# First stage of a hybrid SSD and retention step: dummies of 512 columns, a transfer of their own for the condition vectors, modulation weights first in the queue, no paired modulation

## The chip, the cores and the metric

The kernel runs on one core of a Trainium2 chip. The metric is the device time of that core in microseconds (us). The kernel before takes 601.47 us, the median of three runs (601.31 to 603.59). Its engines are TensorE (PE in the profile, with PEld for its weight loads), VectorE (DVE), ScalarE (ACT), GpSimd (POOL) and SyncE (SP, which here only issues DMAs). ScalarE issues two DMAs too, on a queue of its own.

## The reference, cut to what matters

One layer works on 640 tokens of width 1024: 128 context tokens (modulated by the vector `c_ctx`) and 512 latent tokens (modulated by `c`). The stage that the change touches computes the first two lines below and the part `h @ w_in` for 512 of the columns.

```python
def _layer(x, cond, ...):
    mod = jax.nn.silu(cond) @ w_mod + b_mod
    shift, scale, gate = jnp.split(mod, 3, axis=-1)
    h = _rms(x, norm_pre_w) * (1 + scale[:, None, :]) + shift[:, None, :]
    out, s_ssd, s_ret = _mixer(h.astype(x.dtype), ...)    # begins with u = h @ w_in
    y = x + gate[:, None, :] * _rms(out, norm_post_w)
```

All the rest of the mixer (convolution, two bidirectional scans, gates, the output product with `w_out`) is untouched.

## The kernel before, in words

The tokens lie in five tiles of 128 (t = 0 is the context, t = 1 to 4 the latent tokens), the width in eight k-tiles of 128. The normalised and modulated activations are kept transposed, as a high and a low half (`hh`, `hl`); each product with a weight tile is three matmuls of 512 columns (high by high, high by low, low by high). The first stage fills `hh` and `hl` and at the same time multiplies them with the first 512 columns of `w_in`, into five banks of accumulators (`acc`). It ends when 120 such matmuls are done; then the first product named `gt` begins.

The stage is a list of steps in the string START, whose order is the order in which the program is written down. A letter is a step, the number its k-tile or token tile:

- L loads a token tile (512 KB), M a tile of modulation weights (1 MB), W a tile of `w_in` (256 KB). All go out on SP's queue.
- N squares a token tile on ScalarE and sums it (line 278), then GpSimd raises the sum to the power -1/2 (279). E scales a whole token tile on ScalarE, Q its first 128 columns on VectorE, R the other 896.
- A is the modulation product of a k-tile: eight matmuls with `silc` (SiLU of the condition vectors) as weights, and a copy `ms` on VectorE. B turns the result by two matmuls with the identity (`mod<-idt,ms`) and makes shift and scale (`ash`) on VectorE. P does A for two k-tiles in one bank.
- U and V split a weight tile into `w0h` (ScalarE) and `w0l` (VectorE).
- H transposes token tiles (PE `tr`), modulates them on ScalarE (`h`, line 355) and splits them on VectorE (`hh`, `hl`).
- G is the three matmuls of one token tile and one k-tile. Z are dummy matmuls on zeros: Z1 is four of 128 columns.

Three small tensors come first: `pk` (216 columns of vectors, the condition vectors in columns 0 to 15) and `idt` (the identity) on ScalarE's queue, and the tokens on SP's. `silc` is made of `pk` by one ScalarE and two VectorE instructions (267 to 270). Each engine works through its list in order; a DMA may be issued only when the transfer eight DMAs before it has landed, because eight semaphores go round.

Of the kernel before, what the change touches and what calls it, by code (L numbers as in the profile page):

```python
# [10 lines left out]
F32 = mybir.dt.float32  # L11
F32R = mybir.dt.float32r
AF = mybir.ActivationFunctionType
ALU = mybir.AluOpType
# [3 lines left out]
P = 128  # L18
D = 1024
KT = 8  # L20
# [5 lines left out]
Z0, XS0, B0, C0, DT0, Q0, K0, V0, G0 = 0, 1024, 2048, 2560, 3072, 3104, 3616, 4128, 5152  # L26


PK_CC, PK_C, PK_NPW, PK_BSH, PK_BSC = 0, 8, 16, 24, 32
# [12 lines left out]


START = """
L0 M0 L1 W0 L2 M1 W1 L3 L4 M2 W2
Z18 N0 E0 N1 A0 M3 Z2 B0 H0:0 U0 Q1 V0 W3 Z4 H0:1 N2 G0:0 Z1 G0:1 R1 Q2 R2 A1 M4 U1 H0:2 W4 N3 B1 G0:2 H1:012 V1 Z4 G1:012
Q3 A2 M5 H0:3 R3 N4 U2 W5 G0:3 H1:3 B2 V2 Q4 H0:4 G1:3 R4 H2:0123 G0:4 H1:4 A3 M6 G2:01 G1:4 H2:4 U3 W6 G2:23 B3 V3
P4 M7 H3:0123 G2:4 H3:4 U4 W7 B4 V4
G3:01 H4:0123 H4:4 U5 G3:234 B5 V5 C0
P6 G4:01 H5:0123 H5:4 U6 G4:234 B6 V6 F2  # L50
G5:01 H6:0123 H6:4 U7 G5:234 B7 V7 F2
G6:01 H7:0123 H7:4 F2 G6:234
G7:01234
"""
# [55 lines left out]
def body(ctx, tc, io):  # L110
    nc = tc.nc
    vec, act, pool, sp, pe = nc.vector, nc.scalar, nc.gpsimd, nc.sync, nc.tensor

    def sb(name, bufs=1, side=None):
        return ctx.enter_context(tc.tile_pool(name=name, bufs=bufs, side=side))

    const = sb("const")
# [8 lines left out]
    def mm(out, a, b, start, stop, big=False):  # L126
        r = pe.matmul(out, lhsT=a, rhs=b, start=start, stop=stop)  # L127
        if big:
            last["mm"] = getattr(r, "ins", r)

    def stt(out, in0, s, in1, op0=ALU.mult, op1=ALU.add, eng=vec):
        eng.scalar_tensor_tensor(out=out, in0=in0, scalar=s, in1=in1, op0=op0, op1=op1)  # L132

    def tt(out, a, b, op, eng=vec):
        return eng.tensor_tensor(out=out, in0=a, in1=b, op=op)  # L135

    def bank(name):
        return pi.tile([P, 512], F32, tag="i", name=name)


    pk = const.tile([P, PK_N], F32, name="pk")
    cst = const.tile([P, CN], F32, name="cst")
    idt = const.tile([P, P + 2], F32, name="idt")
    rope = const.tile([P, 4, 2, 64], F32, name="rope")
    act.dma_start(out=pk, in_=io["pk"])
    act.dma_start(out=idt, in_=io["idt"])
    tl = const.tile([P, 1], F32, name="tl")
# [6 lines left out]
    def pkc(base, n=0):  # L154
        return pk[:, base + n:base + n + 1]
# [87 lines left out]
    st_ = tc.alloc_tile_pool(name="st", bufs=1, side="right")  # L243
# [3 lines left out]
    wm_t, w0_t = {}, {}  # L247
# [16 lines left out]

    sc_ = st_.tile([P, KT, 32], F32, name="silc")
    th = st_.tile([P, 16], F32, name="thc")
    act.activation(th, pk[:, PK_CC:PK_CC + 16], AF.Tanh, scale=0.5)
    vec.memset(sc_, 0.0)
    stt(th, th, 1.0, pk[:, PK_CC:PK_CC + 16], ALU.add, ALU.mult)
    vec.tensor_scalar(sc_[:, :, 0:2], th.rearrange("p (c k) -> p k c", c=2), 0.5, None, op0=ALU.mult)  # L270
    bs1 = st_.tile([P, 8], F32, name="bs1")
    vec.tensor_scalar(bs1, pk[:, PK_BSC:PK_BSC + 8], 1.0, None, op0=ALU.add)
# [15 lines left out]
        eng.tensor_scalar(xs_t[t][:, q], xs_t[t][:, q], rs[:, t:t + 1], None, op0=ALU.mult)  # L288

    mods = {}  # L290
    wz = st_.tile([P, P], mybir.dt.bfloat16, name="wz")
    pool.memset(wz, 0.0)

    def warm(n):
        wps = bank("warm")
        for _ in range(4 * n):
            mm(wps[:, 0:P], wz, wz, True, True)

    def mod_a(kt):
        m = bank("mod")  # L300
# [15 lines left out]
    def low0(kt):  # L316
        hi = w0[kt][0]
        lo = st_.tile([P, 512], F32R, tag="w0l", name="w0l", bufs=3)
        tt(lo, w0_t.pop(kt), hi.bitcast(F32), ALU.subtract)
        w0[kt] = (hi, lo)  # L320

    ash_t, h_last = {}, {}

    def mod_pair(kt):
        m = bank("mod")
        for n in range(2):
            wm = wm_t.pop(kt + n)
            for k in range(KT):
                g = 32 * (k % 4)
                mm(m[g:g + 32, n * 256:n * 256 + 256], sc_[:, k, :], wm[:, k, :], k < 4, k >= 4)  # L330
        ms = st_.tile([P, 512], F32, tag="ms2", name="ms2")
        vec.tensor_copy(ms, m)
        for n in range(2):
            mods[kt + n] = (None, ms[:, n * 256:n * 256 + 256])

    def mod_b(kt):
        m, ms = mods.pop(kt)
        if m is None:
            m = bank("modb")
        mm(m[:, 256:258], ms[:, 0:P], idt[:, P:P + 2], True, True)  # L340
        mm(m[:, 258:260], ms[:, P:256], idt[:, P:P + 2], True, True)
        ash = ash_t[kt] = st_.tile([P, 4], F32, tag="ash", name="ash", bufs=3)
        vec.tensor_scalar(ash[:, 0:2], m[:, 256:258], pkc(PK_BSH, kt), None, op0=ALU.add)
        vec.tensor_scalar(ash[:, 2:4], m[:, 258:260], bs1[:, kt:kt + 1], pkc(PK_NPW, kt), op0=ALU.add, op1=ALU.mult)

    def h_tile(kt, ts):
        ash = ash_t[kt]
# [22 lines left out]
    def gemm0(kt, t):  # L370
# [5 lines left out]

    acc = [pg.tile([P, 512], F32, tag="g", name="acc0") for _ in range(5)]
    steps = {
        "M": load_wm, "W": load_w0, "L": load_x, "A": mod_a, "P": mod_pair, "U": high0, "V": low0, "B": mod_b, "N": norm_x,
        "E": all_x, "Q": first_x, "R": rest_x,  # L380
    }
    for op in START.split():
        k = int(op[1:].split(":")[0])
        if op[0] == "H":
            h_tile(k, [int(t) for t in op[3:]])
        elif op[0] == "G":
            for t in op[3:]:
                gemm0(k, int(t))
        elif op[0] == "Z":
            warm(k)  # L390
        elif op[0] == "F":
            feed(k, 0)
        elif op[0] == "C":
            sp.dma_start(out=cst, in_=io["cst"])
            sp.dma_start(out=rope, in_=io["rope"])
        else:
            steps[op[0]](k)
# [562 lines left out]
    for g in range(1, 4):  # L960
        n = clock["slot"]
# [5 lines left out]
    n = clock["slot"]  # L967
# [114 lines left out]
    n = clock["slot"]  # L1082
# [99 lines left out]
```

## Time and profile before

| What | Value |
|---|---|
| Median of three runs | 601.47 us |
| The profiled execution: its own time, and its span | 602.56 us, 600.7 us |
| PE busy / DVE / ACT / POOL | 583.8 / 415.8 / 338.2 / 30.8 us |
| First real matmul of PE (modulation of k-tile 0) | 7.72 us |
| First accumulating matmul | 11.50 us |
| End of the first stage (first `gt`) | 60.17 us |
| DMA rate, 5 to 25 us | 407 to 420 GB/s |

PE is busy for 97% of the span, but a dummy counts as busy too, and a matmul's time in a row is its passage through the array, longer than its share of the issue. What the stage costs is therefore read from the chain of waits, which runs back from the last instruction and names at each step what was waited for. Times are from the span's start.

### The profile page before, as it was taken

Reading aid. Unit: us, or ns where it says so; the run is one execution under the profiler, and the core shown is the slowest. Engines: PE = TensorE matmul, PEld = TensorE weight load, DVE = VectorE, ACT = ScalarE, POOL = GpSimd, SP = SyncE. Lnnn points to the kernel's source line nnn. Section 1 sums busy time; section 2 is a strip of 40 time slices with the busy share of each in tenths; the row PEclk is TensorE's granted clock in tenths of the full one; section 3 lists DMA queues with packets and bytes.
Section 4 is the critical chain, followed back from the end, with each engine's and each line's share of the span. In section 5 each row is a group of like instructions: output and inputs, shape, how many; then the busy total and the mean of one; then the engine's idle time right before and its main releaser. Section 6 shows DMA issues by size and latency. Waiting matters only on the chain.

```text
span 600.7 us, 11145 instructions
## 1 busy us (share of the span) xinstructions
PE 583.8 (97%) x3925; PEld 525.1 (87%) x3925; DVE 415.8 (69%) x938; ACT 338.2 (56%) x935; POOL 30.8 (5%) x112
## 2 busy tenths in 40 slices
PE   7999999999999999999999999999999999999995
PEld 6568989988999998899999888999999777788895
DVE  3648498756789865658897656799767855743665
ACT  5538246664666765465776546566755847262421
POOL 1000002100000010000011000000110000000010
PEclk9999999999999999999999999999999999999998
DMA  8983032643335533332563313355437676384032
GB/s 343 371 314 121 21 106 60 181 131 106 88 114 175 165 92 89 88 105 89 176 179 100 93 56 102 106 178 162 118 101 231 229 243 209 123 274 119 17 141 106
DMA packets 47639, 87.45 MB, mean 146 GB/s; under 512 B 5792, under 2 KB 18656, under 8 KB 46048
## 3 DMA queue, kind: packets, MB, share of 16 engines
q1 hardware_dynamic: 47296, 86.57, 45.5%
q8 instruction: 31, 0.51, 0.3%
q10 hardware_dynamic: 288, 0.18, 0.1%
q14 instruction: 24, 0.20, 0.1%
HBM read 75.03 MB, written 9.60 MB: 141 GB/s over the span
## 4 chain that ended last, share of the span: by engine, by line
PE 70%; DVE 8%; DMA 8%; ACT 7%; issue 4%; POOL 2%; SPq 0%; DVEq 0%; POOLq 0%; ACTq 0%
PE gw L127 24%; PE gc L127 15%; PE gt L127 9%; PE acc L127 5%; PE go L127 4%; DMA cf<-cumd 3%; DMA x<-x 2%; PE ss L127 2%; PE sfb L127 2%; DMA raw<-ws 1%; PE ry L127 1%; PE sy L127 1%; DVE SC L132 1%; DVE wlo L135 1%; PE st L809 1%
## 5 line engine op out<-in xcount | busy, mean ns | idle before, releaser
L135 DVE TENSOR_TENSOR wlo<-raw,whi 128x512 fp32r<-128x512 f32 (+1 forms) x120 | 82.1, 691 | 48.0 <-ACT whi L178 47.2
L178 ACT CAST whi<-raw 128x512 fp32r<-128x512 f32 (+1 forms) x120 | 73.6, 619 | 74.1 <-PE gw L127 45.6
L127 PE MATMUL gc<-hh,whi 128*128 128x320 f32 x384 | 96.8, 331 | 0.0
L127 PE MATMUL gc<-hl,whi 128*128 128x320 f32 x384 | 88.3, 310 | 0.0
L127 PE MATMUL gc<-hh,wlo 128*128 128x320 f32 x384 | 87.7, 310 | 0.0
L127 PEld LDWEIGHTS gc<-hh,whi 128*128 128x128 f32 x384 | 64.0, 189 | 1.1
L127 PEld LDWEIGHTS gc<-hl,whi 128*128 128x128 f32 x384 | 64.4, 188 | 0.1
L127 PEld LDWEIGHTS gc<-hh,wlo 128*128 128x128 f32 x384 | 64.1, 188 | 0.0
L127 PE MATMUL gw<-whi,hh 128*128 128x512 f32 x120 | 50.6, 421 | 0.8 <-ACT u L514 0.8
L127 PE MATMUL gw<-whi,hl 128*128 128x512 f32 x120 | 47.1, 392 | 0.0
L127 PE MATMUL gw<-wlo,hh 128*128 128x512 f32 x120 | 47.0, 391 | 0.0
L127 PE MATMUL gt<-whi,hh 128*128 128x256 f32 (+1 forms) x160 | 46.4, 290 | 0.0
L127 PE MATMUL gt<-wlo,hh 128*128 128x256 f32 (+1 forms) x160 | 45.8, 286 | 0.0
L127 PE MATMUL gt<-whi,hl 128*128 128x256 f32 (+1 forms) x160 | 45.8, 286 | 0.0
L892 ACT ACTIVATE m<-gu,dt 128x128 f32<-128x128 f32 x80 | 31.2, 390 | 16.4 <-DVE gu L135 14.6
L864 ACT ACTIVATE cf<-cf,dmc 128x128 f32<-128x128 f32 x80 | 26.5, 393 | 19.9 <-DMA cf<-cumd 19.9
L135 DVE TENSOR_TENSOR m<-m,cf 128x512 f32<-128x512 f32 x40 | 27.6, 689 | 8.8 <-ACT cf L893 7.6
L127 PE MATMUL gw<-whi,mrh 128*128 128x512 f32 x80 | 32.4, 404 | 0.0
L127 PE MATMUL gw<-wlo,mrh 128*128 128x512 f32 x80 | 31.3, 391 | 0.0
L867 ACT ACTIVATE cf<-cf,ncf 128x128 f32<-128x128 f32 x80 | 26.4, 394 | 8.5 <-DVE cf L135 8.5
L127 PEld LDWEIGHTS gt<-whi,hh 128*128 128x128 f32 x160 | 30.5, 191 | 0.7 <-issue 0.5
L893 ACT ACTIVATE cf<-gu,dt 128x128 f32<-128x128 f32 x80 | 31.0, 387 | 0.0
(238 smaller groups left out, 1334.7 us busy)
## 6 DMA issues: line engine op xcount, KB each, us to landing
raw<-ws SPq DMA_DIRECT2D x116, 256.0 KB, 2.8
cf<-cumd SPq DMA_DIRECT2D x20, 512.0 KB, 4.1
wm<-wm SPq DMA_DIRECT2D x8, 1024.0 KB, 9.1
mraw<-mixd SPq DMA_DIRECT2D x16, 320.0 KB, 3.8
ef<-ecumd SPq DMA_DIRECT2D x32, 128.0 KB, 3.4
wg<-wg SPq DMA_DIRECT2D x4, 1024.0 KB, 6.4
x<-x SPq DMA_DIRECT2D x5, 512.0 KB, 8.1
mixd<-rmix SPq DMA_DIRECT2D x20, 128.0 KB, 2.4
```

The source lines that it names most:

```text
L127: r = pe.matmul(out, lhsT=a, rhs=b, start=start, stop=stop)
L132: eng.scalar_tensor_tensor(out=out, in0=in0, scalar=s, in1=in1, op0=op0, op1=op1)
L135: return eng.tensor_tensor(out=out, in0=a, in1=b, op=op)
L178: act.copy(hi, raw)
L809: pe.transpose(o[:, n], src[:, s], ident)
L864: act.activation(cf[:, e, 1, q], cf[:, e, 1, q], AF.Identity, bias=dmc[:, c, h:h + 1])
L867: act.activation(cf[:, e, 0, q], cf[:, e, 0, q], AF.Exp, bias=ncf[:, c, h:h + 1])
L892: act.activation(m[:, e, q], gu[:, 0], AF.Copy, scale=dt[:, c, h:h + 1])
L893: act.activation(cf[:, e, 1, q], gu[:, 1], AF.Copy, scale=dt[:, c, 16 + h:17 + h])
```

## The change

The transfer of the 16 condition columns is made a DMA of its own (`cc`), ahead of `pk`; the two instructions on `thc` read it instead of `pk`. In START the first loads are now M0 L0 W0 L1 L2 in place of L0 M0 L1 W0 L2. The dummies become matmuls of 512 columns, one for each count of Z in place of four, with new counts. E0 is gone: token tile 0 is scaled by Q0 and R0 like the others. N1 and N2 now stand behind the first U0, Q0 and V0. P is gone; A4 to A7 are separate steps, one ahead of each H. The low half of a weight tile (V) is issued behind `ash` of its k-tile.

```diff
-L0 M0 L1 W0 L2 M1 W1 L3 L4 M2 W2
-Z18 N0 E0 N1 A0 M3 Z2 B0 H0:0 U0 Q1 V0 W3 Z4 H0:1 N2 G0:0 Z1 G0:1 R1 Q2 R2 A1 M4 U1 H0:2 W4 N3 B1 G0:2 H1:012 V1 Z4 G1:012
+M0 L0 W0 L1 L2 M1 W1 L3 L4 M2 W2
+Z14 A0 M3 Z2 B0 N0 U0 Q0 V0 W3 Z9 H0:0 N1 N2 Z3 G0:0 R0 Q1 R1 Z3 H0:1 Z2 A1 M4 U1 Q2 G0:1 R2 H0:2 W4 N3 B1 G0:2 V1 H1:012 N4 Z4 G1:012
...
-P4 M7 H3:0123 G2:4 H3:4 U4 W7 B4 V4
-G3:01 H4:0123 H4:4 U5 G3:234 B5 V5 C0
-P6 G4:01 H5:0123 H5:4 U6 G4:234 B6 V6 F2
+A4 M7 H3:0123 G2:4 H3:4 U4 W7 B4 V4
+A5 G3:01 H4:0123 H4:4 U5 G3:234 B5 V5 C0
+A6 G4:01 H5:0123 H5:4 U6 G4:234 B6 V6 F2
...
+    cc = const.tile([P, 16], F32, name="cc")
+    act.dma_start(out=cc, in_=io["pk"][:, PK_CC:PK_CC + 16])
     act.dma_start(out=pk, in_=io["pk"])
     act.dma_start(out=idt, in_=io["idt"])
...
-    act.activation(th, pk[:, PK_CC:PK_CC + 16], AF.Tanh, scale=0.5)
+    act.activation(th, cc, AF.Tanh, scale=0.5)
     vec.memset(sc_, 0.0)
-    stt(th, th, 1.0, pk[:, PK_CC:PK_CC + 16], ALU.add, ALU.mult)
+    stt(th, th, 1.0, cc, ALU.add, ALU.mult)
...
-    wz = st_.tile([P, P], mybir.dt.bfloat16, name="wz")
+    wz = st_.tile([P, 512], mybir.dt.bfloat16, name="wz")
...
-        for _ in range(4 * n):
-            mm(wps[:, 0:P], wz, wz, True, True)
+        for _ in range(n):
+            mm(wps, wz[:, 0:P], wz, True, True)
...
-            tt(lo, w0_t.pop(kt), hi.bitcast(F32), ALU.subtract)
+        with tc.issue_after(ash_last[kt]):
+            tt(lo, w0_t.pop(kt), hi.bitcast(F32), ALU.subtract)
```

The program is handed to a scheduler, which sets the final order on each engine. On PE the dummies stand as follows now: 14 ahead of the modulation of k-tile 0, 3 behind it, 8 between `mod<-idt,ms` and the first `tr`, 4 ahead of the first `acc`, then 2, 2, 2 and 2; before it was 72, 8, none, 16 and 4, then 9 and 7, each of 128 columns.

On VectorE, the start of the program, before (`thc` and `silc` are the steps of SiLU; `bs`, `cw`, `nrm` are vectors made of `pk`):

```order
L272 TENSOR_SCALAR bs_114<-pk 128x8 [waits DMAHW0_49]
L533 TENSOR_SCALAR cw<-pk 128x64
L635 COPY nrm<-pk 128x8
L636 TENSOR_SCALAR nrm<-pk 128x8
L132 SCALAR_TENSOR_TENSOR thc<-thc,pk 128x16 [waits Activation_49]
L629 TENSOR_SCALAR lamb<-lamb 128x16 [waits Activation_49]
L270 TENSOR_SCALAR silc<-thc 128x8x2 [waits DVE_49]
```

The same place now:

```order
L274 TENSOR_SCALAR bs_116<-pk 128x8 [waits DMAHW2_49]
L523 TENSOR_SCALAR cw<-pk 128x64
L625 COPY nrm<-pk 128x8
L626 TENSOR_SCALAR nrm<-pk 128x8
L132 SCALAR_TENSOR_TENSOR thc<-thc,cc 128x16 [waits DMAHW0_49,Activation_49]
L619 TENSOR_SCALAR lamb<-lamb 128x16 [waits Activation_49]
L272 TENSOR_SCALAR silc<-thc 128x8x2 [waits DVE_49]
```

Nothing moved: `thc` reads `cc` now, but the four instructions on `pk` still stand ahead of it.

On ScalarE, the squares of the token tiles (`hl,ss<-x`) among the first modulated tiles (`h`), before:

```order
L278 ACTIVATE hl,ss<-x 128x1025
L282 ACTIVATE x<-x,rs 128x1024
L278 ACTIVATE hl,ss<-x 128x1025
L355 ACTIVATE h_257<-tr,ash 128x128
L313 CAST w0h<-raw_133 128x512
L355 ACTIVATE h_287<-tr,ash 128x128
L278 ACTIVATE hl,ss<-x 128x1025
```

The same place now:

```order
L280 ACTIVATE hl,ss<-x 128x1025
L315 CAST w0h<-raw_132 128x512
L345 ACTIVATE h_209<-tr,ash 128x128
L280 ACTIVATE hl,ss<-x 128x1025 x2
L345 ACTIVATE h_233<-tr,ash 128x128
L315 CAST w0h<-raw_142 128x512
L345 ACTIVATE h_262<-tr,ash 128x128
```

The squares of token tiles 1 and 2 stand behind the first `h` now (tile 1's stood ahead of it), and both ahead of the second `h`.

On VectorE, from the first `hh` to the second (`hh` and `hl` of a token tile; `x<-x,rs` of 128 columns is Q, of 896 is R), now:

```order
L348 CAST hh<-h_209 128x128
L135 TENSOR_TENSOR hl<-h_209,hh 128x128
L290 TENSOR_SCALAR x<-x,rs 128x896
L290 TENSOR_SCALAR x<-x,rs 128x128
L290 TENSOR_SCALAR x<-x,rs 128x896
L290 TENSOR_SCALAR x<-x,rs 128x128
L290 TENSOR_SCALAR x<-x,rs 128x896
L348 CAST hh<-h_233 128x128
L135 TENSOR_TENSOR hl<-h_233,hh 128x128
L308 COPY ms<-mod 128x256
```

Before, only `w0l` stood between these two pairs; Q2 and R2 (the last two scalings here) came behind the second pair.

## Rows read from the trace of the kernel before

**Rows 1.** Page, its first line.

```profile
span 600.7 us, 11145 instructions
```

**Rows 2.** Chain of waits, 0 to 100 us: start us, us, what.

```profile
0.72 4.33 DMA pk<-pk
...
5.44 11.30 DMA x<-x
...
16.83 0.95 ACT hl L278
...
18.63 0.29 DVE x L288
...
19.24 2.36 PE acc L127 x9
21.60 1.04 PE mod L127 x16
...
23.88 0.97 PE acc L127 x3
...
24.95 0.32 PE tr L351
...
26.06 1.66 PE acc L127 x6
...
27.84 1.00 PE mod L127 x16
...
32.63 1.34 PE mod L127 x20
...
54.66 5.51 PE acc L127 x24
60.17 16.00 PE gt L127 x120
```

**Rows 3.** Timeline, 0 to 17 us: start, us, engine, line, operation, tiles [idle before].

```profile
5.08 0.17 DVE L272 TENSOR_SCALAR bs<-pk 128x8 f32<-128x8 f32 x1 [3.93 <-DMA pk<-pk]
...
5.61 0.18 DVE L270 TENSOR_SCALAR silc<-thc 128x16 f32<-128x16 f32 x1
...
6.01 1.04 ACT L278 ACTIVATE hl<-x 128x1025 fp32r<-128x1025 f32 x1
...
7.72 1.07 PE L127 MATMUL mod<-wm,silc 128*32 128x256 f32 x16 [1.27 <-DMA wm<-wm]
...
9.33 0.61 PE L127 MATMUL mod<-idt,ms 128*128 128x2 f32 x4
...
11.50 0.49 PE L127 MATMUL acc<-w0h,hh 128*128 128x512 f32 x1
...
12.55 0.68 DVE L288 TENSOR_SCALAR x<-x,rs 128x896 f32<-128x896 f32 x1
...
14.86 1.07 PE L127 MATMUL mod<-wm,silc 128*32 128x256 f32 x16 [1.21 <-DMA wm<-wm]
...
16.23 0.46 ACT L355 ACTIVATE h<-tr,ash 128x128 f32<-128x128 f32 x1
```

**Rows 4.** DMA queues, 2.50 to 4.57 us: packets, MB, share of 16 engines.

```profile
q1 hardware_dynamic: 139, 0.61, 72.0%
q10 hardware_dynamic: 144, 0.11, 23.0%
```

**Rows 5.** DMA issues, ScalarE's queue: KB, us from issue to landing.

```profile
idt<-idt ACTq DMA_DIRECT2D x1, 65.0 KB, 6.6
```

**Rows 6.** Stretches: length, PE busy (instructions), granted clock, DMA share, GB/s.

```profile
2.00:3.00 1.00, 1.00 (x12) 1.00 0.59 152
4.00:5.00 1.00, 1.00 (x21) 1.00 1.06 425
594.00:595.00 1.00, 0.12 (x1) 1.00 0.00 0
597.00:598.00 1.00, 0.00 (x0) 0.79 0.29 111
```

More of the change, by code (lines that the diff above doesn't have):

```diff
@@ L44 @@
 START = """
-L0 M0 L1 W0 L2 M1 W1 L3 L4 M2 W2
-Z18 N0 E0 N1 A0 M3 Z2 B0 H0:0 U0 Q1 V0 W3 Z4 H0:1 N2 G0:0 Z1 G0:1 R1 Q2 R2 A1 M4 U1 H0:2 W4 N3 B1 G0:2 H1:012 V1 Z4 G1:012
-Q3 A2 M5 H0:3 R3 N4 U2 W5 G0:3 H1:3 B2 V2 Q4 H0:4 G1:3 R4 H2:0123 G0:4 H1:4 A3 M6 G2:01 G1:4 H2:4 U3 W6 G2:23 B3 V3
-P4 M7 H3:0123 G2:4 H3:4 U4 W7 B4 V4
-G3:01 H4:0123 H4:4 U5 G3:234 B5 V5 C0
-P6 G4:01 H5:0123 H5:4 U6 G4:234 B6 V6 F2
-G5:01 H6:0123 H6:4 U7 G5:234 B7 V7 F2
+M0 L0 W0 L1 L2 M1 W1 L3 L4 M2 W2
+Z14 A0 M3 Z2 B0 N0 U0 Q0 V0 W3 Z9 H0:0 N1 N2 Z3 G0:0 R0 Q1 R1 Z3 H0:1 Z2 A1 M4 U1 Q2 G0:1 R2 H0:2 W4 N3 B1 G0:2 V1 H1:012 N4 Z4 G1:012
+Q3 A2 M5 H0:3 R3 U2 W5 G0:3 H1:3 B2 V2 Q4 H0:4 G1:3 R4 H2:0123 G0:4 H1:4 A3 M6 G2:01 G1:4 H2:4 U3 W6 G2:23 B3 V3
+A4 M7 H3:0123 G2:4 H3:4 U4 W7 B4 V4
+A5 G3:01 H4:0123 H4:4 U5 G3:234 B5 V5 C0
+A6 G4:01 H5:0123 H5:4 U6 G4:234 B6 V6 F2
+A7 G5:01 H6:0123 H6:4 U7 G5:234 B7 V7 F2
 G6:01 H7:0123 H7:4 F2 G6:234
@@ L318, in low0 @@
         lo = st_.tile([P, 512], F32R, tag="w0l", name="w0l", bufs=3)
-        tt(lo, w0_t.pop(kt), hi.bitcast(F32), ALU.subtract)
+        with tc.issue_after(ash_last[kt]):
+            tt(lo, w0_t.pop(kt), hi.bitcast(F32), ALU.subtract)
         w0[kt] = (hi, lo)
[L322 to L334, printed above, removed]
+    ash_t, ash_last, h_last = {}, {}, {}
     def mod_b(kt):
         m, ms = mods.pop(kt)
-        if m is None:
-            m = bank("modb")
         mm(m[:, 256:258], ms[:, 0:P], idt[:, P:P + 2], True, True)
@@ L343, in mod_b @@
         vec.tensor_scalar(ash[:, 0:2], m[:, 256:258], pkc(PK_BSH, kt), None, op0=ALU.add)
-        vec.tensor_scalar(ash[:, 2:4], m[:, 258:260], bs1[:, kt:kt + 1], pkc(PK_NPW, kt), op0=ALU.add, op1=ALU.mult)
+        r = vec.tensor_scalar(ash[:, 2:4], m[:, 258:260], bs1[:, kt:kt + 1], pkc(PK_NPW, kt), op0=ALU.add, op1=ALU.mult)
+        ash_last[kt] = getattr(r, "ins", r)
     def h_tile(kt, ts):
@@ L378, in body @@
     steps = {
-        "M": load_wm, "W": load_w0, "L": load_x, "A": mod_a, "P": mod_pair, "U": high0, "V": low0, "B": mod_b, "N": norm_x,
+        "M": load_wm, "W": load_w0, "L": load_x, "A": mod_a, "U": high0, "V": low0, "B": mod_b, "N": norm_x,
         "E": all_x, "Q": first_x, "R": rest_x,
```

## The prediction

> **What bounds the kernel now.** I read the page's first line for the span [rows 1], then the chain of waits over the first 100 us [rows 2], then the timeline of the first 17 us for what feeds the chain [rows 3], and last the DMA queues [rows 4, 5]. In the chain the reader should see one border. From 27.84 us to 60.17 us every piece belongs to PE: modulation, transposes and the 120 accumulating matmuls follow each other without a wait. Before 27.84 us PE is waited for or waits. So whatever the change does to the first stage counts only through the moment at which PE becomes solid; after it the same matmuls must be done in either kernel (the unpaired modulation issues as many as the paired one, 16 each), and everything behind 60.17 us moves with it.
>
> What sets that moment is also in the chain: token tile 3 lands at 16.74 us (5.44 + 11.30), its square runs at 16.83, it is scaled at 18.63, and nine accumulating matmuls of k-tile 1 start at 19.24 [rows 2]. I call 19.24 the mark. From the mark to 27.84 PE loses 1.24 us (22.64 to 23.88) and 0.79 us (25.27 to 26.06) to its exchange with ScalarE and VectorE. The forecast is the new time of the mark, plus what changes in those two waits.
>
> **The part that decides: the queue of ScalarE.** Before, `pk` is the first transfer on that queue and lands at 5.05 us (0.72 + 4.33) [rows 2]; `idt`, issued 0.45 us later, needs 6.6 us [rows 5] and lands at about 7.77. The cause is in the packets: from 2.50 to 4.57 us ScalarE's queue (q10) moved 144 packets, and SP's (q1) 139 [rows 4]. That is one for one, though a packet of q10 carries 0.11 MB / 144, under 1 KB, and one of q1 over 4 KB. 144 is `pk`, 128 rows and 16 closing writes. So a transfer on q10 costs about as many turns as it has rows, whatever its size, and each turn waits for a large packet of q1.
>
> `cc` has 128 rows too. It takes the place of `pk`, and `pk` takes the place of `idt`. What q1 moves beside them is the same 1.5 MB, with the modulation weights ahead of the token tile. I therefore put `pk` at 7.77 us, the time at which the second transfer of that queue lands now. The bounds: at best 5.5 (5.05 plus one issue of 0.45), if `cc` costs no turns; at worst about 8.2 (7.77 and the issue).
>
> [...]
>
> `cc` itself is of no use where it stands. `thc` could start on it, but on VectorE the four instructions on `pk` stand ahead of it, as the order shows, so `silc` still follows `pk`: 5.08 to 5.79 before [rows 3], 0.74 us after the landing.
>
> **The path to the mark, step by step** (times of the new kernel with `pk` at 7.77):
>
> - `silc` is done at 8.51. The weights of k-tile 0 have landed by then: now they land just before 7.72 behind a token tile [rows 3], and they go first. The modulation starts at 8.55 (7.72 before), takes 1.00 (piece at 27.84) to 9.55. Having the weights first gains nothing, as `silc` is later.
> - Three dummies of 512 columns: 0.23 each, taken from the accumulating matmuls of the same width (5.51 / 24) [rows 2]; 0.69, to 10.24. The two turning products take 0.34 (1.34 for 20 matmuls less 1.00 for 16): 10.58.
> - Eight dummies before the first `tr`: 1.84, to 12.42. They are not covered: what else `tr` waits for is ready. The square of tile 0 follows 0.93 us after the first instruction on `pk` (5.08 to 6.01 [rows 3]), so 8.73; from a square to the scaled tile's start it is 1.80 (16.83 to 18.63); and the scaling stands behind `ash`, at about 11.3, to 11.6. Cost of the dummies here: 0.8 us. Before, none stood there.
> - First accumulating matmul: 1.11 after the transpose (24.95 to 26.06), 13.53, against 11.50. The first `h` starts 0.37 after `tr` (14.86 + 1.00 to 16.23), at 12.79, and takes 0.46.
> - Squares of tiles 1 and 2 now stand behind it: 13.25 and, 1.15 later (1.04 and the read of the sum), 14.4. Both tiles landed long ago. Scaling of tile 2: 14.4 + 1.80 = 16.2.
> - On VectorE the second `hh` stands behind that scaling and the 896-column one (0.68 [rows 3]): with 0.15 to 0.3 for the short instructions around it, matmul G0:1 starts about 1.0 after 16.2, at 17.2. Three matmuls, 0.69.
> - PE's modulation of k-tile 1 stands behind G0:1: 17.9, against 14.86. There it waited for its weights; now the weights wait for it.
> - On ScalarE the square of tile 3 stands behind the `h` of tile 2, which needs the transposes behind that modulation: 1.37 + 0.46 less 0.1 of overlap, 19.6. Its landing at 16.74 is no longer the limit. From there to the mark 2.41 as before (16.83 to 19.24): 22.0.
>
> The mark moves by +2.8 us. After it the order on PE is the same, with one change on VectorE: `ash` now goes ahead of `hh` of tile 3 and of `w0l`, and `ash` waits for the turning product (0.61 [rows 3]). That is between nothing and 0.6, in the first of the two waits; I take 0.3. In the solid part A5, A6 and A7 go singly between G steps; their bank is free by then, cost 0, at most 0.2 each if `hh` is late. Fewer and longer dummies change nothing elsewhere, since PE would wait there. The wider `wz` delays the first dummy by some tenths; 14 of them end near 6 us, before anything real. Semaphores of the DMAs: SP's sixth to ninth DMAs now wait for `cc`, the weights, `pk` and `idt`, up to about 9 us, but 1.5 MB is queued ahead of each, so the DMA engines do not run dry.
>
> **The sum.** +2.8 + 0.3 = +3.1 us. The profiled execution took 602.56 us (a span of 600.7 and 1.9 around it), 1.09 above the median; it would become 605.7, and the median 601.47 becomes 604.6. A difference under 0.5% (3.0 us) I call no change, as a measurement of this kernel can tell no less; the forecast lies on that border.
>
> **The rivals.**
>
> *The clock falls.* After the 14 dummies PE idles from about 6 to 8.55 us. At the end of the kernel the last matmul is in 594 to 595, and the granted clock falls within 597 to 598 (0.79, so from 1.00 to 0.50 inside it) [rows 6], after the engine had stood idle for 3 to 4 us. Idle stretches of 1.27 and 1.21 us [rows 3] did no harm. Ours, 2.5 us, lies between. [...] At the start 12 dummies ran per us, then 21 from 4 us on [rows 6], after some 2.6 us of work; half of 2.6 is lost at most, 1.3 us: 605.9. [...]
>
> *`pk` lands early*, at 5.5. For it: q10's packets are small. Against: rows 4. Then `silc` is ready at 6.24, the weights land near 6.2 (an estimate: 7.7 less 512 KB at 400 GB/s), the modulation starts at 6.3, and dummies and products run to 10.2 in place of 12.42. All that follows is 2.2 us earlier, the mark is at 19.8: +0.6 + 0.3, 602.4.
>
> *The two waits behind the mark go*, the rival for a kernel that is not slower. `w0l` no longer stands between `ms` and `hh`; if that was what PE waited for in 22.64 to 23.88, and the second wait closes with it, 2.0 us come back and the 0.3 is not paid. With `pk` early: 600.1; with `pk` late 602.3. It decides if `hh` can start right after `ms`. Against it: `hh` now stands behind `ash`.
>
> **How the numbers follow.** Forecast, `pk` late and the dummies in the way: 50%, 603.4 to 605.8. The clock falls on top of it: 12%. `pk` early: 28%. The waits go: 5% with `pk` early, 5% with it late. Nothing in the trace lets PE gain 3 us: the two waits are 2.0 in all. So faster has 3%, for what I overlook; slower by over 0.5% takes a little more than half of the forecast's chance, the clock case and some overrun, 43%; 54% lie within 0.5%. The range goes from 601.4 to 606.2 and leaves the smaller half of the last rival and the overruns out.
>
> **What would show it.** `pk` landing between 7.3 and 8.2 and `cc` not before 5; `silc` within 0.8 us after `pk`; the first `tr` right behind eight dummies near 12.4; the modulation of k-tile 1 near 17.9 with no wait for its weights; the first matmul of k-tile 1 on tile 0 near 22; PE solid from about 31; first `gt` near 63.3. The forecast is wrong if `pk` lands before 6.5, if the modulation of k-tile 1 starts before 16, or if the pieces between the mark and 27.84 shorten by more than 1 us.

## The result: slower by 7 us, twice what was forecast

The changed kernel took 611.12 us (median of 6 runs, 608.07 to 613.1) beside 603.02 us for the kernel before: ratio 1.0135, 95% interval [1.0108, 1.0162], some 8.1 us. Measured once more later it took 608.63 us, ratio 1.0100 [1.0080, 1.0121], some 6.0 us. The forecast was +3.1 us, its range ended at +4.7. (Ratios leave out executions that were disturbed.)

The page of the changed kernel begins with the span, against 600.7 [rows 1]; its own time was 611.89 us:

```profile
span 610.1 us, 10986 instructions
```

The chain of waits of the changed kernel (start us, us, what), which answers to [rows 2]; the last two lines belong to the later part of the trace:

```profile
15.89 0.88 DVE x L290 x2
...
16.96 0.96 PE acc L127 x3
17.92 1.79 PE mod L127 x16
...
23.44 2.35 PE acc L127 x9
...
32.35 1.00 PE mod L127 x16
...
58.98 5.54 PE acc L127 x24
64.52 5.59 PE gt L127 x42
...
117.17 5.71 DMA cf<-cumd
...
540.32 6.13 DMA mraw<-mixd
```

Read it in three parts. The mark is at 23.44 instead of 19.24, +4.20. From there to the first `gt` little is added: 64.52 against 60.17, +4.35. But the span is 9.4 us longer, so 5.0 us more are lost behind the first stage, where the change touches nothing. `cf<-cumd` took 4.36 us before and 5.71 now; at 540 us `mraw<-mixd` took 6.13 us, while none of its six transfers took over 4.1 before, and PE then waits 2.0 us. The kernel before had there (chain of waits, then the shortest, the median and the longest of the six transfers of `mraw`):

```profile
112.81 4.36 DMA cf<-cumd
...
DMA to landing us min/median/max: 2.8/3.7/4.0
```

The same instruction comes +4.35 us later at 60 us, +5.7 at 119, +6.8 at 492 and +8.9 at 540 us (times of the kernel before).

The timeline of the changed kernel in the first 18 us (start, us, engine, line, operation, tiles [idle before]) answers to [rows 3]:

```profile
7.54 0.17 DVE L274 TENSOR_SCALAR bs<-pk 128x8 f32<-128x8 f32 x1 [6.39 <-DMA pk<-pk]
...
8.07 0.17 DVE L272 TENSOR_SCALAR silc<-thc 128x16 f32<-128x16 f32 x1
...
8.30 1.07 PE L127 MATMUL mod<-wm,silc 128*32 128x256 f32 x16 [2.30 <-DVE silc L272]
...
12.42 0.46 ACT L345 ACTIVATE h<-tr,ash 128x128 f32<-128x128 f32 x1 [2.31 <-PE tr L341]
12.78 1.05 ACT L280 ACTIVATE hl<-x 128x1025 fp32r<-128x1025 f32 x1
...
13.19 0.50 PE L127 MATMUL acc<-w0h,hh 128*128 128x512 f32 x1
...
17.85 1.86 PE L127 MATMUL mod<-wm,silc 128*32 128x256 f32 x16
```

`bs`, the first instruction on `pk`, starts at 7.54, not at 5.08; the square in front of which everything queues stands behind the first `h`; and the modulation of k-tile 1 starts at 17.85. Its 1.86 us in place of 1.07 is the clock. The stretches of the changed kernel (PE, PEld, DVE, ACT, POOL busy, granted clock, DMA share, GB/s):

```profile
16.00:17.00 1.00, 0.04 (x1) 0.04 (x1) 0.96 (x4) 0.24 (x1) 0.00 (x0) 1.00 1.00 418
17.00:18.00 1.00, 1.00 (x7) 0.59 (x11) 0.23 (x1) 0.00 (x0) 0.00 (x0) 0.99 1.02 426
18.00:19.00 1.00, 1.00 (x12) 0.44 (x9) 0.00 (x0) 0.00 (x0) 0.00 (x0) 0.50 1.02 391
21.00:22.00 1.00, 1.00 (x5) 0.53 (x6) 0.56 (x4) 0.65 (x2) 0.27 (x1) 0.80 1.02 395
```

PE works in pieces from 13.65 us on and does next to nothing between 16 and 17; then the granted clock goes to 0.50 just before 18 us and comes back between 21 and 22.

### The profile page after: what moved, and what is told of

Same layout as the page of the kernel before. It is cut to its first block, busy times and chain, and to the rows that moved or that the text cites. A ratio compares the mean times of both kernels' runs of the same rounds, so it can differ in the third digit from the quotient of the medians.

```text
span 610.1 us, 10986 instructions
## 1 busy us (share of the span) xinstructions
PE 586.9 (96%) x3845; PEld 521.9 (86%) x3846; DVE 416.9 (68%) x942; ACT 337.6 (55%) x934; POOL 31.3 (5%) x112
## 4 chain that ended last, share of the span: by engine, by line
PE 68%; DVE 9%; ACT 8%; DMA 6%; issue 4%; POOL 2%; POOLq 0%; DVEq 0%; SPq 0%; ACTq 0%
PE gw L127 21%; PE gc L127 15%; PE gt L127 9%; PE acc L127 5%; PE go L127 4%; DMA cf<-cumd 4%; DMA mraw<-mixd 2%; PE ss L127 2%; PE mod L127 2%; PE sfb L127 2%; PE ry L127 1%; DVE SC L132 1%; DVE wlo L135 1%; PE sy L127 1%; PE st L799 1%
```

## The experiments

Three questions: which edit moves the mark, what drops the clock, and where 2 to 5 us behind the first stage come from. For the last, one view gave the idea. The DMA queues of the changed kernel from 105 to 116.5 us (packets, MB, share of 16 engines; then KB and us to landing):

```profile
q8 instruction: 1, 0.02, 0.6%
...
cumd<-ct SPq DMA_DIRECT2D x1, 80.0 KB, 3.3
ecumd<-ce SPq DMA_DIRECT2D x1, 80.0 KB, 2.7
```

In the kernel before (105 to 116.5 us as well) no q8 packet is near, and `cumd` takes 1.7 us:

```profile
cumd<-ct SPq DMA_DIRECT2D x1, 80.0 KB, 1.7
```

I take q8, whose kind the profile calls "instruction", to bring PE's code, by its count: the page has 30 such packets of 16 KB (0.49 MB) for 7,691 matmuls and weight loads, one for 256. Below, "fetch" stands for a packet of q8. Within 114.1 to 115.3 us this packet has 5.7% of 16 engines, that is 1.1 us of one engine (0.057 x 16 x 1.2), and I take it that the share of `cumd` that lies on that engine waits for it. The change has 158 PE instructions fewer (79 dummies, each a matmul and a weight load), so every later fetch falls on other work. I call this the code theory; the rival is scatter from one execution to the next.

### First three

Without `cc`:

```diff
-    act.dma_start(out=cc, in_=io["pk"][:, PK_CC:PK_CC + 16])
...
-    act.activation(th, cc, AF.Tanh, scale=0.5)
+    act.activation(th, pk[:, PK_CC:PK_CC + 16], AF.Tanh, scale=0.5)
...
```

> The changed kernel without the transfer of cc: thc reads pk again, and pk is first on ScalarE's queue. Queue theory (the transfer cc costs the first stage 2.2 us or more, as everything up to the mark stands behind pk): pk lands near 5.1, silc near 5.8, the modulation of k-tile 0 starts when its weights land, near 6.5; first tr near 10.3, the mark near 21 or earlier, the first gt near 61.5 against 64.5 in the changed kernel; time 3 us below the changed kernel. Rival (the dummies and the order of squares set the mark, pk does not): the mark stays at 23 and the time within 1 us of the changed kernel. Rival on the later 4.9 us (the shift of TensorE's code fetches against the transfers): the kernel has as many PE instructions as the changed one, so part of the loss behind the first gt stays, though moved; if it is scatter of single executions, it is as likely gone as not.

Measured: 607.76 us, ratio 1.0108 [1.0076, 1.0140]. `pk` lands at 6.16, not 5.1 (beside it SP's queue now moves the 1 MB of weights; in the changed kernel, which has them first too, that queue carries 0.40 MB in 49 packets from 2.75 to 3.75 us, some 8 KB in each, against some 4 KB in [rows 4]), modulation of k-tile 0 at 6.95, k-tile 1 at 16.51 in place of 17.85, and the clock stays up (1.00 in every microsecond from 3 to 24). Chain of waits of this kernel:

```profile
21.16 2.34 PE acc L127 x9
...
62.20 7.86 PE gt L127 x59
```

Of the 2.3 us by which the mark is earlier than 23.44, 1.3 are `cc` (17.85 to 16.51), not 2.2; the other 1.0 is the clock, which did not fall here. Behind `gt` most of the loss is still there, with the fetch again on `cumd` (3.5 us).

The count of the kernel before, in the changed kernel:

```diff
-        for _ in range(n):
-            mm(wps, wz[:, 0:P], wz, True, True)
+        c, w = (93, 77) if n == 14 else (n, 512)
+        for _ in range(c):
+            mm(wps[:, 0:w], wz[:, 0:P], wz[:, 0:w], True, True)
```

> The changed kernel with its first block of 14 dummies of 512 columns written as 93 of 77 columns: the same columns, and as many PE instructions in all as the kernel before has. Code theory: stage 1 as in the changed kernel (first gt 64.0 to 65), but the fetches stand again beside the work where they stood before, and the 4.9 us behind the first gt go: time 606 to 607.5. Rival (scatter, or another edit): time 609 to 612, as the changed kernel.

Measured: 604.50 us, ratio 1.0044 [1.0025, 1.0062], better than either theory said. The first `gt` came at 62.03, since the scheduler, seeing other dummies, had also put the square of tile 1 ahead of the first `h`. Chain of waits:

```profile
20.91 2.36 PE acc L127 x9
...
62.03 7.99 PE gt L127 x60
```

Two things changed, so later kernels take them apart. The texts below call this kernel the third experiment.

`cc` in the kernel before:

```diff
+    cc = const.tile([P, 16], F32, name="cc")
+    act.dma_start(out=cc, in_=io["pk"][:, PK_CC:PK_CC + 16])
     act.dma_start(out=pk, in_=io["pk"])
...
-    act.activation(th, pk[:, PK_CC:PK_CC + 16], AF.Tanh, scale=0.5)
+    act.activation(th, cc, AF.Tanh, scale=0.5)
...
```

> The kernel before plus the transfer of cc first on ScalarE's queue, thc and silc on cc. Queue theory: pk lands near 7.5 instead of 5.05 and idt near 8.4, silc at 8.2, the modulation of k-tile 0 near 8.3 instead of 7.72, first tr 0.5 to 1 us later than before; the squares are free of it, and the mark hangs on the landing of token tile 3 as before (16.8 to 17.2): mark 19.2 to 20, first gt 60.2 to 61, time within 1.5 us of the kernel before. Rival (a late pk costs its whole 2.5 us whatever the order is): first gt 62.5, time 604.

Measured: 602.67 us, ratio 1.0023 [1.0008, 1.0038]. `pk` at 7.48, modulation at 8.27, `tr` at 10.72 (9.80 before), and yet first `gt` at 60.34 (+0.17). The mark does not hang on token tile 3 any more, though: the tile landed at 16.47, and the chain of waits runs from the mark back to `pk`:

```profile
1.16 6.32 DMA pk<-pk
...
19.45 2.35 PE acc L127 x9
```

In that order the path from a late `pk` is only 0.2 us longer at the mark than the path from tile 3 was before (19.45 against 19.24): the rest of the 2.4 us by which `pk` is later falls into slack.

### Second four: count, clock, order

The changed kernel with 93 dummies of 16 columns in the first block:

```diff
-        for _ in range(n):
+        c, w = (93, 16) if n == 14 else (n, 512)
+        for _ in range(c):
```

> The changed kernel with its first 14 dummies of 512 columns written as 93 of 16 columns: as many PE instructions as the kernel before, and on every other engine the same order as the changed kernel (in the third experiment one square also moved). Code theory: the first stage as in the changed kernel, first gt 63.5 to 65 (the clock may come up or fall elsewhere, as the dummies have fewer columns), but the 4.9 us behind it shrink to under 1.5: time 606 to 608. Rival (the gain of the third experiment came from the moved square alone): the loss behind first gt stays at 4 to 5 us, time 610 to 612.

Measured: ratio 1.0121 [1.0092, 1.0151], time 609.75 us in the profiled execution. Behind the narrow dummies PE was slow at a granted clock of 1.00 (9 to 10 us): its first modulation took 1.93 us instead of 1.07. The clock fell once more near 19 us (0.51 from 19 to 20), and first `gt` is at 66.63. But behind it only some 0.8 us are lost, with the order on ScalarE, VectorE and GpSimd the same as in the changed kernel. The total lies between the two forecasts, the trace says "code".

The kernel before with long dummies everywhere (174 instructions fewer, other engines in the same order):

```diff
-        for _ in range(4 * n):
-            mm(wps[:, 0:P], wz, wz, True, True)
+        for _ in range(n):
+            mm(wps.rearrange("p (a b) -> p a b", a=4), wz, wz.unsqueeze(1).to_broadcast([P, 4, P]), True, True)
```

> The kernel before with its 116 dummies of 128 columns written as 29 of 512 (read four times over the same 128 columns), 174 fewer PE instructions, the order on all other engines the same. Code theory: first gt within 0.5 us of 60.1, and yet 2 to 5 us lost behind it, at the transfers near 110 and 540 us on which a code fetch then falls: time 603.5 to 606.5. Rival (the later loss comes from other edits or is scatter): time within 1.5 us of the kernel before.

Measured: 603.73 us, ratio 1.0034 [1.0013, 1.0054]: 3.5 us lost behind the first stage by the median, as the code theory said, but the first stage 1.45 us *shorter*, which neither had. Chain of waits:

```profile
17.79 2.37 PE acc L127 x9
...
58.72 11.33 PE gt L127 x85
```

In the profiled execution itself 1.9 us are lost behind it, nearly all at `cf`: 6.23 us in place of 4.36, with a fetch at 115.5 us in its midst. Why the first stage is shorter the DMA rows from 3 to 16.8 us show, first the kernel before:

```profile
q8 instruction: 1, 0.02, 0.5%
...
x<-x SPq DMA_DIRECT2D x3, 512.0 KB, 10.2
```

then this one, which has no q8 packet there:

```profile
wm<-wm SPq DMA_DIRECT2D x4, 1024.0 KB, 10.6
x<-x SPq DMA_DIRECT2D x3, 512.0 KB, 8.7
```

In the kernel before the first fetch comes at 11.2 us, in the middle of the loading, and token tile 3 lands at 16.74; here it lands at 14.97. In the seven traces with a fetch between 9 and 14 us tile 3 lands at 16.2 to 16.8, in the eight with no fetch before 20 us at 15.0 to 15.2; the half-block kernel below has 15.04 with a fetch at 14.7, just before the landing.

More dummies before G0:1 in the changed kernel:

```diff
-... G0:0 R0 Q1 R1 Z3 H0:1 Z2 A1 M4 ...
+... G0:0 R0 Q1 R1 Z3 H0:1 Z8 A1 M4 ...
```

> The changed kernel with 8 instead of 2 dummies of 512 columns ahead of G0:1, where PE stands idle for 1.28 us before its clock falls; order elsewhere the same. Sparse-work theory (the clock fell to 0.5 from 17.98 to 21.40 us because PE did little between 13.65 and 16.96): the clock stays at 1.00, modulation of k-tile 1 takes 1.07 again instead of 1.86, the mark 22 instead of 23.44, first gt near 63.1 (64.5 in the changed kernel), time 609 to 610. Rival (the idle stretch of 2.3 us from 6.0 to 8.3 us caused the fall, later): the clock falls as in the changed kernel and first gt is 64.5 to 66.

Measured: 607.51 us, ratio 1.0090 [1.0073, 1.0107]. The clock stays at 1.00 in the profiled execution and the modulation takes 1.07 again. Stretch and chain of this kernel:

```profile
18.00:19.00 1.00, 1.00 (x18) 0.43 (x11) 0.04 (x1) 0.00 (x0) 0.00 (x0) 1.00 1.04 399
```

```profile
22.47 2.34 PE acc L127 x9
...
63.59 6.53 PE gt L127 x49
```

The mark without the fall is 22.47; the fall costs 1.0 us. That the six dummies kept the clock up is not shown: further below the changed kernel itself keeps it, without them.

The square of tile 1 ahead of the first `h`, with the changed kernel's count:

```diff
-... N0 U0 Q0 V0 W3 Z9 H0:0 N1 N2 Z3 ...
+... N0 U0 Q0 N1 V0 W3 Z9 H0:0 N2 Z3 ...
...
+                with tc.issue_after(sq_last[1]):
+                    act.activation(h32, tr[:, 0:P], AF.Identity, ...)
...
```

> The changed kernel with the square of token tile 1 ahead of the h of tile 0 on ScalarE (and the scaling of tile 1 so earlier on VectorE): the order that the third experiment had, with the changed kernel's count of PE instructions. Order theory (the squares behind h make a late pk cost what it costs): modulation of k-tile 1 starts near 16.3 instead of 17.85, the clock does not fall, first gt near 61.9 instead of 64.5; the loss of 4 to 5 us behind it stays, as the count is that of the changed kernel: time 607.5 to 609. Rival (the order of squares does not matter, the third experiment gained by its count): first gt 64 to 65, time as the changed kernel.

Measured: 608.02 us, ratio 1.0097 [1.0072, 1.0122]. Chain of waits:

```profile
20.88 2.32 PE acc L127 x9
...
61.95 8.13 PE gt L127 x61
```

The order of squares carries 1.6 us of the mark (22.47 to 20.88). The kernel with 93 dummies of 77 columns has this very order on ScalarE, VectorE and GpSimd and `gt` at 62.03; beside it this one is 3.5 us slower by the medians, while the spans of the profiled executions are 604.2 and 603.1. On PE only the dummies differ.

### Third four: a scan of the count on the kernel before, and two losses undone together

Only the first block of dummies in the kernel before is cut otherwise: 18 of 512 columns, 36 of 256, or 100 of 92 in place of 72 of 128. The last of the three:

```diff
-        for _ in range(4 * n):
-            mm(wps[:, 0:P], wz, wz, True, True)
+        c, w = (100, 92) if n == 18 else (4 * n, P)
+        for _ in range(c):
+            mm(wps[:, 0:w], wz, wz[:, 0:w], True, True)
```

> The kernel before with only its first block of 72 dummies of 128 columns written as 18 of 512, 108 fewer PE instructions, order on the other engines the same. Code theory: the fetch at 11.2 us of the kernel before moves to 16 to 20 us, weights of k-tile 1 land near 13.3 instead of 14.77 and first gt is at 58.5 to 59.5 instead of 60.2, as in the kernel with all dummies long; what the later fetches cost depends on where they fall, 0 to 3 us. Time 600 to 604; the loss or gain behind first gt shows at transfers that a fetch falls on. Rival (the first stage of the all-long kernel gained by its later short blocks): first gt 60.2.

Measured: 602.35 us, ratio 1.0002 [0.9986, 1.0017]; its trace gives no row that can be compared.

> As the previous kernel, but the first block as 36 dummies of 256 columns, 72 fewer PE instructions. Code theory: the first fetch at 14.5 to 17 us, first gt 58.5 to 60.5 by what it falls on; time 599.5 to 604, and different from the previous kernel by what the fetches near 110, 480 and 540 us hit. Rival (fetches cost nothing): time as the kernel before within 0.5 us.

Measured: 601.80 us beside 602.61, ratio 0.9974 [0.9951, 0.9997], the one kernel that beats the kernel before, by an interval just clear of 1; its profiled execution has the same span, 600.7 us. First `gt` at 58.95; the first fetch at 14.7.

> As the two before, but the first block as 100 dummies of 92 columns, 56 more PE instructions than the kernel before. Code theory: the first fetch near 9 us, still inside the loading of the first weights and tiles, first gt 59 to 60.5; every later fetch some 4 us earlier against the work; time 600 to 604. Rival: time as the kernel before within 0.5 us.

Measured: 603.78 us, ratio 1.0029 [1.0010, 1.0047]; first `gt` 59.79, 2 us lost behind it. The same dummy columns cut otherwise move the time by 0.55%.

The changed kernel with both of the first edits, no `cc` and 93 dummies of 77 columns:

```diff
-    act.dma_start(out=cc, in_=io["pk"][:, PK_CC:PK_CC + 16])
...
+        c, w = (93, 77) if n == 14 else (n, 512)
```

> The changed kernel with two of its losses undone together: the count of PE instructions of the kernel before (93 dummies of 77 columns in the first block, which also sets the square of tile 1 ahead of the first h) and no transfer of cc, so pk first on its queue. What is left of the change: weights of k-tile 0 first, the dummies ahead of the first tr, the unpaired modulation, the low halves behind ash. My theory (those cost nothing, cc and the order of squares and the code fetches cost it all): pk lands near 6, modulation of k-tile 0 near 6.9, first gt 60.0 to 61, time 601.5 to 603. Rival (a single modulation or the dummies cost 1 to 2 us by themselves): first gt 61.5 to 62, time 603.5 to 605.

Measured: 604.27 us, ratio 1.0026 [1.0012, 1.0040]. First `gt` at 61.02, as my theory had it; the time lies between the two forecasts. Modulation of k-tile 0 starts at 6.94, that of k-tile 1 at 15.35, the mark is at 20.00: what is left of the change costs 0.8 us and gains nothing. Chain of waits:

```profile
20.00 2.33 PE acc L127 x9
...
61.02 9.06 PE gt L127 x68
```

### Last four: is it scatter?

The first three are kernels from above, unchanged; the fourth is the one with the early square and one more line:

```diff
+        c, w = (39, 184) if n == 14 else (n, 512)
```

> The changed kernel once more, beside the three that follow on one chip. Code theory: time 609 to 611.5; first gt at 64 to 64.7 with the clock falling near 18 us again; 4 to 5 us lost behind it. Rival (the later loss is scatter of single executions): another profile loses it at other places, or loses 0 to 2 us.

Measured: 608.63 us, ratio 1.0100. The clock did *not* fall in this execution of the very same kernel (1.00 from 16 to 19 us), and its chain reads:

```profile
22.29 2.34 PE acc L127 x9
...
63.33 6.79 PE gt L127 x51
...
115.97 4.65 DMA cf<-cumd
...
536.61 6.12 DMA mraw<-mixd
```

The fetch now misses `cumd` (1.7 us to landing), `cf` takes 4.65 us and 0.3 us are lost there; at 540 us a fetch falls on `mraw` again, 6.12 us. Behind the first stage 2.1 us are lost, not 5.0. Both theories hold a part: the place at 540 us repeats, the place at 119 us does not. It does not hang on the clock: without `cc` and with the early square the clock stayed up and the fetch fell on `cumd` (3.5 and 3.2 us).

> The kernel with the square of tile 1 early and the changed kernel's count of PE instructions, once more. Code theory: 3 to 4 us above the next kernel, whose first gt is the same to 0.1 us and which differs in the count alone: time 607 to 608.5. Rival (scatter): within 1 us of the next kernel.

Measured: 606.36 us, ratio 1.0078 [1.0054, 1.0102]; the clock fell between 27.2 and 30.6 us in its profile (0.50 from 28 to 29), first `gt` 63.07.

> The kernel with 93 dummies of 77 columns (same order, count of the kernel before), once more: 604 to 605 by the code theory, within 1 us of the previous kernel by the rival.

Measured: 605.00 us, ratio 1.0052 [1.0035, 1.0068]. The pair differs by 1.4 us, in which the clock has a part; less than I expected, and the intervals overlap. By the medians of both pairs the count is worth 1.4 to 3.5 us; behind the first `gt` of the profiled executions, where the clock has no part, 1.1 and 2.0.

> The same order again with a third count: 39 dummies of 184 columns in the first block, 108 PE instructions fewer than the kernel before. Code theory: what is lost behind the first gt follows from the count whatever the rest of the kernel is, so it is what the kernel before lost with 108 fewer (about 1 us): first gt 61.8 to 62, time 604 to 605.5. Rival (the loss comes from the changed stage and not from the count): time 607 to 608.5, as with 158 fewer.

Measured: 604.75 us, ratio 1.0056 [1.0037, 1.0076], first `gt` 61.99: as forecast from the count alone. (The "about 1 us" in that forecast took for the kernel with 18 dummies of 512 columns a first `gt` that no trace shows.)

All kernels with a trace that can be compared stand in the table. The first `gt` is that of the profiled execution against 60.17. What is lost behind it is given twice: by the median (ratio less 1 times the time of before, less the first `gt`'s difference) and in the profiled execution itself (span less first `gt`, against 600.7 less 60.17). The first mixes many executions with one, and holds what the clock did in the others; the second is of one execution only.

| PE instructions against before | kernel | first `gt` | lost behind it, by the median | in the profiled execution |
|---|---|---|---|---|
| 0 | before + `cc` / 93x77 / again / no `cc` too / 93x16 | +0.2 / +1.9 / +1.9 / +0.8 / +6.5 | 1.2 / 0.8 / 1.3 / 0.7 / 0.8 | -0.8 / 0.5 / 0.2 / 1.0 / 0.8 |
| +56 | before, 100x92 | -0.4 | 2.1 | 1.9 |
| -72 | before, 36x256 | -1.2 | -0.3 | 1.2 |
| -108 | changed, square early, 39x184 | +1.8 | 1.5 | -0.7 |
| -146 | changed, Z8 | +3.4 | 2.0 | 1.9 |
| -158 | changed / again / no `cc` / square early / again | +4.4 / +3.2 / +2.0 / +1.8 / +2.9 | 3.8 / 2.9 / 4.5 / 4.1 / 1.8 | 5.0 / 2.1 / 3.8 / 1.7 / 2.2 |
| -174 | before, all long | -1.5 | 3.5 | 1.9 |

The loss goes with the count and not with the edits of the first stage: with the old count five measurements of four kernels lose 0.7 to 1.3 us by the median and at most 1.0 in the profiled execution, those with 146 to 174 fewer 1.8 to 4.5 and 1.7 to 5.0. That is shown, though the loss does not grow evenly with the difference (39 dummies of 184 columns, 108 fewer, lose least in the profiled execution); and the clock does not explain it: in none of these executions does it fall between the first `gt` and the last matmul. Part of the way from count to loss is shown too. In the five traces in which a fetch falls on `cumd` it takes 2.7 to 3.6 us, in the ten without one 1.7 (2.1 where a fetch began 0.6 us before it). `cf` took 5.7 to 6.2 us in four traces, each with a fetch on `cumd` or on `cf` itself, and these four lose 1.4 to 1.9 us from the first `gt` to the matmul behind `cf` (`rz`, at 119.43 us before), the others at most 0.6. That each microsecond is one fetch on one transfer is not shown: in the first execution of the early-square kernel and in the one with Z8 `cumd` was late (3.2 and 2.7 us) and `cf` was not; and the third `mraw` transfer, the one near 540 us, took 3.4 to 5.8 us in the nine traces with no fetch on it (5.8 in the first execution with 93 dummies of 77 columns) and 4.2 to 6.1 in the seven with one, so what is lost there stays open.

## Why the prediction was wrong

**`pk` behind `cc`: right.** 7.52 us against 7.77 forecast; `cc` itself landed at 5.96, so its rows did cost turns (the changed kernel, 0.5 to 5.5 us):

```profile
pk<-pk ACTq DMA_DIRECT2D x1, 108.0 KB, 6.4
...
cc<-pk ACTq DMA_DIRECT2D x1, 8.0 KB, 5.2
```

8 KB in 5.2 us. The rival of an early `pk` is out. The 144 beside 139 packets of [rows 4] could not decide this, since longer turns, several packets of one queue and then several of the other, would give the same counts over 2 us; the changed kernel does. While `cc` passes, q10 and q1 move 48 and 49 packets from 2.75 to 3.75 us and 55 and 55 in the next microsecond: one for one in each stretch, about three per engine on the mean of 16, and a packet of q1 holds some 8 KB there (0.40 MB in 49).

**The path to the mark: right.** Forecast and trace: modulation 8.55 and 8.30, first matmul on `acc` 13.53 and 13.19, second square 13.25 and 12.78, G0:1 17.2 and 16.96, modulation of k-tile 1 17.9 and 17.85. With the clock up the mark came at 22.29 and 22.47 (22.0 forecast) and first `gt` at 63.33 and 63.59 (63.3). That the repeated execution fits to 0.1 us is in part luck: the mark came 0.3 to 0.5 later than forecast, and the wait behind it grew by 0.1 to 0.2 where 0.3 had been put in. The +3.1 us of the first stage are there, and the experiments part the mark's: 1.3 `cc`, 1.6 the squares behind `h`, 0.8 the rest, together 0.5 more than the 3.2 found. The first two overlap: with the square early, `cc` costs 0.9 (20.88 to 20.00), and both together 2.5 (22.47 to 20.00).

**The clock: right in size, wrong in place and chance.** The rival had 1.3 us for it; it costs 1.0 to 1.2. That 1.3 us is half of 2.6 was the author's estimate and no run shows it: in the changed kernel the clock stood at 0.50 for 3.4 us, and the modulation in it took 1.86 us instead of 1.07. The prediction put the fall behind the 14 dummies, where PE idled for 2.3 us and nothing happened. It came after 13.65 to 16.96 us, where PE works in pieces, behind the long path on VectorE that the prediction itself had worked out. And it comes in some executions only: what decides between two of the same kernel is not shown.

**The step that failed: "everything behind 60.17 us moves with it", with "Fewer and longer dummies change nothing elsewhere, since PE would wait there".** True of the work, but not of the time: the sum put nothing for the stretch behind 60.17 us, and 5.0 us were lost there in the first profiled execution and 2.1 in the second. With 158 PE instructions fewer all later code fetches shift; that the loss comes with the count is shown (at most 1.0 us in the profiled executions with the old count, 1.7 to 5.0 with 158 fewer). That a fetch makes it, the trace of the first execution bears out for the 1.4 us at `cf`, behind a late `cumd`; for the rest it is argued. With the clock, which the sum had only as a rival, this makes up what the forecast lacked. The same step also hid a gain that was to be had: the kernel before loses some 1.4 us at the mark to its own fetch at 11.2 us, an estimate from the kernel with long dummies, which has no fetch from 3 to 16.8 us and its mark at 17.79 in place of 19.24.

**The two waits behind the mark: right not to count on them.** From the mark to the first `gt` it is 40.93 us before, 41.08 after (41.04 when repeated), so they did not close; 0.3 had been put in for `ash`.

## What to carry to other kernels

Look in the DMA rows for a queue that goes with an engine's instructions (here q8, one packet for 256 of PE's) before calling a stretch untouched: this edit took 158 instructions from the busiest engine, the later fetches fell on other transfers, and the time that came with the count (1.7 to 5.0 us) was about as large as what the edit did to the first stage (3.2 to 4.4). So compare two versions at the same count, or scan the count by cutting warm-up dummies otherwise; one cut of three gained 0.26%, which the interval only just tells from nothing. And the place of `cc`, 8 KB, in its queue was paid by `pk` behind it, which landed 2.4 to 2.5 us later; what that cost hung on the order of the work that uses it (1.3 us in the changed order, 0.9 with the square early, 0.2 in the kernel before).

## What the hardware showed that was not expected

- A 16 KB packet on the queue whose count goes with PE's instructions (30 for 7,691) held one DMA engine for 1.1 us (changed kernel, 114.1 to 115.3 us), and an 80 KB transfer on which one fell took 2.7 to 3.6 us instead of 1.7. In the loading of the first stage, where the transfers stand one behind the other, token tile 3 landed 1.1 to 1.8 us later (at 16.2 to 16.8 us with a fetch between 9 and 14 us, at 15.0 to 15.2 without).
- The granted clock of one and the same kernel fell to 0.50 near 18 us in one execution and not in another; a kernel with other squares had its fall at 27.2 us once and none the time before. One fall costs about 1 us there.
- A transfer of 8 KB in 128 rows beside a loaded queue took 5.2 us.
